# Front loads reordered, decay weights in small tiles, identity products first, the memory norm spread over w_out

## The chip, the cores and the metric

One core of a Trainium2 chip runs the whole kernel. The metric is the time of one execution on the device in microseconds (us); the median of three runs before the change is 1790.62.

## What is computed

The reference is one step of a layer of a hybrid streaming encoder, for 512 prompt tokens and 8 x 16 sample tokens with the same weights, D = 1024, fp32:

```
h = RMSNorm(x);  z = h @ w_in, cut by columns into
  A: band attention (8 heads x 64),   B: gated delta net (4 heads, 128 x 128 state),
  C: Mamba-2 scan (16 heads x 64),    three merge gates g_A, g_B, g_C
x += w_out( sig(g_A) P_A(y_A) + sig(g_B) P_B(y_B) + sig(g_C) P_C(y_C) )
x += CrossAttention(RMSNorm(x), keys and values of RMSNorm(memory))
x += w_down( u * silu(conv(v)) ),  [u, v] = RMSNorm(x) @ w_up
y = RMSNorm(x)
RMSNorm(x) = x * rsqrt(mean(x^2) + eps) * gain
```

The outputs are y, the new attention and memory keys and values, and the states of B, C and the convolutions. Only w_in's column blocks, the normalizations and the last product of w_down are touched by the change.

## The kernel before

The 640 tokens are 5 tiles of 128; D is 8 slices (k) of 128. TensorE (PE) multiplies numbers in fp32r, so every fp32 weight tile is split into a high and a low part: the high part `wh` is a copy by ScalarE (`act`, L249), the low part `wl = raw - wh` a subtraction by GpSimd or VectorE (`tt`, L243). Activations are split in the same way (xTh, xTl). Each product is then three: high by high, low by high, high by low. A weight tile arrives in a "raw" slot (two of them, 512 KB each), its parts lie in "wh"/"wl" slots (six each) or, with `loose=True`, in the general pool "U" of 41 buffers. "Q" is a pool of 16 small tiles (128 x 128). PSUM has two "D" tiles of two banks and four "P" tiles of one bank.

All loads are issued by SyncE (SP) in program order, with a bounded number in flight. The order of the instructions on each engine is fixed when the program is built, by a scheduler that starts from the program's order; inside it, dense parts are generators ("units", `add`, `need`, `drive`) from which the main sequence takes pieces to fill waits.

What the change touches, in the order of the run:

- The front of `run` (from L1801): x tile 0 is loaded, then the gain, then the first four k slices of the V columns of w_in (two raw tiles, `raws`), then x tiles 1 to 4. Tile 0 is normalized and transposed (`norm_T`, L516 on), then tiles 1 and 2, then 3 and 4. Between these, the splits of the V weights are issued. `norm_T` squares x on ScalarE with an accumulated sum (written "junk"), makes 1/rms by 14 short VectorE operations (`inv_rms`: v, y, w, then t, t, y three times), multiplies (xn), transposes xn on PE into PSUM (nps) and copies the parts xTh (ScalarE) and xTl (VectorE). `rel_table` copies the relative bias table, 1 MB as broadcast.
- `decays` (L597): three narrow column blocks of w_in, 32 columns in all, are loaded into one tile "rawd" out of the two raw slots, and PE multiplies them as they are (dps). It is a unit between the first two attention units; aqk is the copy of their products from PSUM, which PE then transposes (t5a).
- `c_norm` (L1207): the outputs yc of branch C are scaled by 1/rms (ScalarE for even token tiles, VectorE for odd ones), transposed (cn, four "P" tiles at a time) and split into ych, ycl. Pieces of a queued unit are taken at its `yield`s; the gate products (gps) of branch C's merge follow.
- `mem_norm` (L1539): the two tiles of memory tokens are normalized ahead of the w_out products (`add_proj`).
- `last_proj` (L1769): the last product of w_down (dn). Its first 512 columns are done first, then x times the final gain on GpSimd for the five token tiles, then the weights of the second 512 columns are split, half of them in loose tiles.

Of the kernel before, what the change touches and what calls it, by code (L numbers as in the profile page):

```python
# [7 lines left out]
F32 = mybir.dt.float32  # L8
F32R = mybir.dt.float32r
I32 = mybir.dt.int32  # L10
AF = mybir.ActivationFunctionType
ALU = mybir.AluOpType
# [21 lines left out]
LQ = 1  # L34
QUARTERS = ((0, 256), (256, 256), (512, 256), (768, 256))
# [9 lines left out]
class Enc:  # L45
# [202 lines left out]
    def act(self, out, in_, f=AF.Copy, **kw):  # L248
        self.nc.scalar.activation(out, in_, f, **kw)  # L249
# [347 lines left out]
    def decays(self, X):  # L597
        nc = self.nc
        w = self.I["w_in"][0]
        raw = self.wp.tile([P, 8, 32], F32, name="rawd", tag="raw", bufs=2)  # L600
        wv = w.rearrange("(k p) c -> p k c", p=P)

        for c, c0, n in ((0, 3072, 8), (8, 6152, 16), (24, 3080, 8)):
            self.load(raw[:, :, c:c + n], wv[:, :, c0:c0 + n])

        ps = self.PD("dps")
        for i in range(2):
            for p in range(2):
                for js in range(2):
                    for j in range(4):  # L610
                        k = 2 * j + i
                        self.mm(ps[32 * j:32 * j + 32, js, :HALF], raw[:, k, :],
# [594 lines left out]
    def c_norm(self, ys, Y):  # L1207
# [4 lines left out]
        yield FN  # L1212
# [326 lines left out]
    def mem_norm(self):  # L1539
        g = self.grow(self.I["norm_mem"][0])  # L1540
        T = [[self.U("mT" + a, F32R, (P, 2, 256)) for _ in range(4)] for a in "hl"]
        for t in range(2):
# [4 lines left out]
            s = slice(t * P, (t + 1) * P)  # L1547
            r = self.token_norm([x])
            for j, ps in self.norm_tile(x, r, g):
                for i in range(2):  # L1550
                    self.act(T[0][2 * j + i][:, :, s], ps[:, 2 * i:2 * i + 2, :])
                for i in range(2):
                    self.tt(T[1][2 * j + i][:, :, s], ps[:, 2 * i:2 * i + 2, :],
                            T[0][2 * j + i][:, :, s].bitcast(F32), ALU.subtract)
        self.MX = [(T[0][k // 2][:, k % 2, :], T[1][k // 2][:, k % 2, :]) for k in range(NK)]

# [212 lines left out]
    def last_proj(self, w, H, x, k0, nk):  # L1769
# [4 lines left out]
        yield from self.add_proj(w, H, x, k0=k0, nk=nk, nm="dn", cols=((0, 512),))  # L1774
# [3 lines left out]
        wk = [a for k in range(0, nk, 2) for a in self.weights(w, 512, 512, k0 + k, 2, (nc.vector, nc.gpsimd), loose=k >= 4)]  # L1778
# [20 lines left out]
    def run(self):  # L1799
# [6 lines left out]
        x0 += [self.load_x(t) for t in range(1, NT)]  # L1806
        self.ident = self.C("ident", [P, P])
        make_identity(self.nc, self.ident)
        self.masks()
# [3 lines left out]
        for c, t in ((0, 1), (1, 3)):  # L1813
            for a in range(2):
                wv += self.split_w(raws[a] if c == 0 else self.raw(w, 1024, 512, 4 + 2 * a, 2), 2, 512, loose=c == 0)
# [9 lines left out]
        self.rel_table()  # L1825
        self.need("A0")
        with self.tc.issue_after(self.last_raw.ins):
            self.loads()
# [168 lines left out]
```

## Time and profile before

| | before |
|---|---|
| runs (us) | 1790.62, 1787.3, 1790.74 |
| median | 1790.62 |
| profiled execution | 1787.08, span 1785.4 |
| mean granted clock of PE | 0.981 |
| PE busy | 1683.1 (94%) |
| VectorE (DVE) busy | 860.4 (48%) |
| ScalarE (ACT) busy | 650.5 (36%) |
| GpSimd (POOL) busy | 607.4 (34%) |
| DMA | 181.78 MB, mean 102 GB/s |

The busy times are sums over the span. PE is busy nearly all of it, so time can come from the stretches in which it waits or runs at a lower clock. Times in the rows below are from the start of the span.

### The profile page before, as it was taken

Reading aid. Unit: us, or ns where it says so; the run is one execution under the profiler, and the core shown is the slowest. Engines: PE = TensorE matmul, PEld = TensorE weight load, DVE = VectorE, ACT = ScalarE, POOL = GpSimd, SP = SyncE. Lnnn points to the kernel's source line nnn. Section 1 sums busy time; section 2 is a strip of 40 time slices with the busy share of each in tenths; the row PEclk is TensorE's granted clock in tenths of the full one; section 3 lists DMA queues with packets and bytes.
Section 4 is the critical chain, followed back from the end, with each engine's and each line's share of the span. In section 5 each row is a group of like instructions: output and inputs, shape, how many; then the busy total and the mean of one; then the engine's idle time right before and its main releaser. Section 6 shows DMA issues by size and latency. Waiting matters only on the chain.

```text
span 1785.4 us, 32450 instructions
## 1 busy us (share of the span) xinstructions
PE 1683.1 (94%) x12925; PEld 1542.6 (86%) x12925; DVE 860.4 (48%) x1762; ACT 650.5 (36%) x1596; POOL 607.4 (34%) x641
## 2 busy tenths in 40 slices
PE   5898999999999998999999899999889999999997
PEld 4687778898988898998899889987789989998995
DVE  5046762446787674755434463243574404431433
ACT  4234543433434432343342245342443313321332
POOL 3252232123322353453432326201144434443432
PEclk9999999999999999999999999999989999999999
DMA  5332156322222334335323345146332222222221
GB/s 177 89 80 66 40 174 197 131 68 64 78 78 67 109 107 113 85 99 145 84 60 119 106 130 166 59 166 236 114 100 74 83 71 83 72 74 82 72 94 61
DMA packets 232749, 181.78 MB, mean 102 GB/s; under 512 B 14321, under 2 KB 198646, under 8 KB 232470
## 3 DMA queue, kind: packets, MB, share of 16 engines
q1 hardware_dynamic: 210672, 165.74, 30.5%
q10 hardware_dynamic: 21926, 13.96, 2.5%
q8 instruction: 102, 1.67, 0.4%
q14 instruction: 49, 0.40, 0.1%
HBM read 163.09 MB, written 16.06 MB: 100 GB/s over the span
## 4 chain that ended last, share of the span: by engine, by line
PE 69%; DVE 10%; DMA 4%; ACT 3%; issue 2%; POOL 1%; ACTq 0%; SPq 0%; POOLq 0%; DVEq 0%
PE ups L235 9%; PE fps L235 9%; PE gps L235 8%; PE dn L235 8%; PE pps L235 6%; PE ap L235 5%; PE tm L235 4%; PE qps L235 3%; PE cps L235 2%; DVE xc L246 2%; PE bps L235 2%; PE pl L235 1%; DVE t L243 1%; PE py L235 1%; PE xkt L240 1%
## 5 line engine op out<-in xcount | busy, mean ns | idle before, releaser
L243 POOL TENSOR_TENSOR wl<-raw,wh 128x512 fp32r<-128x512 f32 x373 | 490.8, 1321 | 961.3 <-ACT wh L249 791.3
L249 ACT ACTIVATE wh<-raw 128x512 fp32r<-128x512 f32 x400 | 248.8, 629 | 591.0 <-PE fps L235 93.8
L246 DVE SCALAR_TENSOR_TENSOR xc<-xp,vec,xc 128x664 f32<-128x664 f32 (+1 forms) x116 | 117.4, 1012 | 3.2
L235 PE MATMUL gps<-xTh,wh 128*128 128x320 f32 x448 | 117.4, 340 | 0.0
L235 PE MATMUL gps<-xTh,wl 128*128 128x320 f32 x448 | 106.3, 315 | 0.0
L235 PE MATMUL gps<-xTl,wh 128*128 128x320 f32 x448 | 105.6, 315 | 0.0
L568 DVE TENSOR_SCALAR xc<-xp,vec 128x656 f32<-128x656 f32 (+1 forms) x34 | 32.2, 948 | 131.9 <-ACT xp L249 131.9
L235 PE MATMUL dn<-wl,hh 128*128 128x512 f32 x220 | 86.4, 394 | 2.9 <-POOL wl L243 2.6
L235 PE MATMUL dn<-wh,hh 128*128 128x512 f32 x220 | 86.3, 393 | 0.1
L235 PE MATMUL dn<-wh,hl 128*128 128x512 f32 x220 | 85.8, 391 | 0.0
L235 PEld LDWEIGHTS gps<-xTh,wh 128*128 128x128 f32 x448 | 74.1, 192 | 12.0 <-issue 10.8
L235 PE MATMUL fps<-fTh,wh 128*128 128x320 f32 x352 | 82.3, 311 | 0.0
L235 PE MATMUL ups<-fTh,wl 128*128 128x320 f32 x352 | 82.0, 310 | 0.0
L235 PE MATMUL fps<-fTl,wh 128*128 128x320 f32 x352 | 81.9, 310 | 0.0
L235 PE MATMUL fps<-fTh,wl 128*128 128x320 f32 x352 | 81.9, 310 | 0.0
L235 PE MATMUL ups<-fTl,wh 128*128 128x320 f32 x352 | 81.8, 310 | 0.0
L235 PE MATMUL ups<-fTh,wh 128*128 128x320 f32 x352 | 81.7, 310 | 0.0
L235 PEld LDWEIGHTS gps<-xTh,wl 128*128 128x128 f32 x448 | 76.0, 190 | 1.0 <-issue 0.8
L235 PEld LDWEIGHTS gps<-xTl,wh 128*128 128x128 f32 x448 | 76.1, 191 | 0.7 <-issue 0.6
L235 PE MATMUL tm<-wh,xTh 128*128 128x256 f32 (+1 forms) x200 | 65.5, 327 | 8.6 <-ACT wh L249 4.4
L243 DVE TENSOR_TENSOR x<-x,dn 128x512 f32<-128x512 f32 x30 | 19.3, 683 | 108.1 <-PE dn L235 107.7
L235 PE MATMUL tm<-wh,xTl 128*128 128x256 f32 (+1 forms) x200 | 63.6, 318 | 0.2 <-DVE xTl L243 0.2
(521 smaller groups left out, 4434.5 us busy)
## 6 DMA issues: line engine op xcount, KB each, us to landing
raw<-in_w_in_dram SPq DMA_DIRECT2D x72, 512.0 KB
raw<-in_w_up_dram SPq DMA_DIRECT2D x44, 512.0 KB
raw<-in_w_down_dram SPq DMA_DIRECT2D x22, 512.0 KB
ck<-in_cache_attn_k_dram SPq DMA_DIRECT2D x32, 256.0 KB
cv<-in_cache_attn_v_dram SPq DMA_DIRECT2D x32, 256.0 KB
xck<-in_cache_mem_k_dram SPq DMA_DIRECT2D x32, 256.0 KB
xcv<-in_cache_mem_v_dram SPq DMA_DIRECT2D x32, 256.0 KB
raw<-in_wx_o_dram SPq DMA_DIRECT2D x14, 512.0 KB
```

The source lines that it names most:

```text
L235: self.nc.tensor.matmul(out, lhsT=lhsT, rhs=rhs, start=start, stop=stop)
L240: self.nc.tensor.transpose(out, in_, self.ident[b:b + k, b:b + k])
L243: return (eng or self.nc.vector).tensor_tensor(out, a, b, op=op)
L246: self.nc.vector.scalar_tensor_tensor(out, a, s, b, op0=op0, op1=op1)
L249: self.nc.scalar.activation(out, in_, f, **kw)
L568: nc.vector.tensor_scalar(acc[:, :n], xp[:, :n], taps[0], bias, op0=ALU.mult, op1=ALU.add)
```

## The change

Five parts:

1. In `run`, the other four k slices of the V weights are loaded right behind x tile 1, into four "U" tiles `rawv`, ahead of x tiles 2 to 4; their splits are issued on ScalarE and GpSimd behind the last ScalarE instruction of tile 0. The relative table is loaded behind the first A0 weights.
2. 14 products of the identity with itself come first on PE.
3. `decays` uses two "Q" tiles and six loads in place of one "raw" tile and three loads.
4. `c_norm` takes 6.5 us' worth of pieces, not 3, at its first `yield`, and one unit of gate products (GD) is queued for it.
5. `mem_norm` is a generator whose steps are spread over w_out's products; `last_proj` splits the weights of its second half ahead of the last k slice of its first half, all but the first two slices in loose tiles.

```diff
--- before.py
+++ after.py
@@ -32,6 +32,7 @@
 LS, LC, LX = 3, 3, 3
 SEQ = (0, 1, 2, 4, 3)
 LQ = 1
+NWARM = 14
 QUARTERS = ((0, 256), (256, 256), (512, 256), (768, 256))
 SKA = 1
 MAGIC = float(0x5F3759DF)
@@ -246,7 +247,7 @@
         self.nc.vector.scalar_tensor_tensor(out, a, s, b, op0=op0, op1=op1)
 
     def act(self, out, in_, f=AF.Copy, **kw):
-        self.nc.scalar.activation(out, in_, f, **kw)
+        self.last_act = self.nc.scalar.activation(out, in_, f, **kw)
 
     def load(self, out, in_):
         return self.nc.sync.dma_start(out, in_)
@@ -597,11 +598,12 @@
     def decays(self, X):
         nc = self.nc
         w = self.I["w_in"][0]
-        raw = self.wp.tile([P, 8, 32], F32, name="rawd", tag="raw", bufs=2)
+        raw = [self.qp.tile([P, 4, 32], F32, name=self.nm("rawd"), tag="Q") for _ in range(2)]
         wv = w.rearrange("(k p) c -> p k c", p=P)
 
         for c, c0, n in ((0, 3072, 8), (8, 6152, 16), (24, 3080, 8)):
-            self.load(raw[:, :, c:c + n], wv[:, :, c0:c0 + n])
+            for i in range(2):
+                self.load(raw[i][:, :, c:c + n], wv[:, 4 * i:4 * i + 4, c0:c0 + n])
 
         ps = self.PD("dps")
         for i in range(2):
@@ -609,7 +611,7 @@
                 for js in range(2):
                     for j in range(4):
                         k = 2 * j + i
-                        self.mm(ps[32 * j:32 * j + 32, js, :HALF], raw[:, k, :],
+                        self.mm(ps[32 * j:32 * j + 32, js, :HALF], raw[k // 4][:, k % 4, :],
                                 X[k][p][:, js * HALF:(js + 1) * HALF].bitcast(F32),
                                 start=(i == 0 and p == 0), stop=(i == 1 and p == 1))
             yield 2.2
@@ -1209,7 +1211,7 @@
         st = self.SM("cst", [P, NT])
         nc.vector.tensor_reduce(st, self.css.rearrange("p a b -> p b a"), axis=AX.X, op=ALU.add)
         r = self.rsqrt(st, 0.25 / D, EPS)
-        yield FN
+        yield 6.5
         for g in range(2):
             for t in (4, 0, 1, 2, 3):
                 if t % 2:
@@ -1537,22 +1539,39 @@
 
 
     def mem_norm(self):
+
         g = self.grow(self.I["norm_mem"][0])
         T = [[self.U("mT" + a, F32R, (P, 2, 256)) for _ in range(4)] for a in "hl"]
+        self.MX = [(T[0][k // 2][:, k % 2, :], T[1][k // 2][:, k % 2, :]) for k in range(NK)]
+
+        def put(t, j, xn):
+            s = slice(t * P, (t + 1) * P)
+            ps = self.PP("nps")
+            for i in range(4):
+                self.tr(ps[:, i * P:(i + 1) * P], xn[:, i * P:(i + 1) * P])
+            ps = ps.rearrange("p (a b) -> p a b", b=P)
+            for i in range(2):
+                self.act(T[0][2 * j + i][:, :, s], ps[:, 2 * i:2 * i + 2, :])
+            for i in range(2):
+                self.tt(T[1][2 * j + i][:, :, s], ps[:, 2 * i:2 * i + 2, :],
+                        T[0][2 * j + i][:, :, s].bitcast(F32), ALU.subtract)
+
+        todo = []
         for t in range(2):
             x = []
             for j in range(2):
                 x.append(self.U("mx", shape=(P, 512)))
                 self.load(x[j], self.I["mem_prompt"][0, t * P:(t + 1) * P, j * 512:(j + 1) * 512])
-            s = slice(t * P, (t + 1) * P)
             r = self.token_norm([x])
-            for j, ps in self.norm_tile(x, r, g):
-                for i in range(2):
-                    self.act(T[0][2 * j + i][:, :, s], ps[:, 2 * i:2 * i + 2, :])
-                for i in range(2):
-                    self.tt(T[1][2 * j + i][:, :, s], ps[:, 2 * i:2 * i + 2, :],
-                            T[0][2 * j + i][:, :, s].bitcast(F32), ALU.subtract)
-        self.MX = [(T[0][k // 2][:, k % 2, :], T[1][k // 2][:, k % 2, :]) for k in range(NK)]
+            for j in range(2):
+                xn = self.U("xn", shape=(P, 512))
+                self.stt(xn, x[j], r, g[j], ALU.mult, ALU.mult)
+                todo.append((t, j, xn))
+            yield
+            for a in todo:
+                put(*a)
+                yield
+            todo = []
 
     def mem_kv(self):
         I, O = self.I, self.O
@@ -1771,11 +1790,14 @@
         nc, O = self.nc, self.O
         g = self.grow(self.I["norm_final"])
         ss = self.SM("fss", [P, 2, NT])
-        yield from self.add_proj(w, H, x, k0=k0, nk=nk, nm="dn", cols=((0, 512),))
+        gen = self.add_proj(w, H, x, k0=k0, nk=nk, nm="dn", cols=((0, 512),))
+        for _ in range(nk - 1):
+            yield next(gen)
+        wk = [a for k in range(0, nk, 2) for a in self.weights(w, 512, 512, k0 + k, 2, (nc.vector, nc.gpsimd), loose=k >= 2)]
+        yield from gen
         for t in range(NT):
             self.sumsq(x[t][0], ss[:, 0, t:t + 1])
             self.tt(x[t][0], x[t][0], g[0], ALU.mult, nc.gpsimd)
-        wk = [a for k in range(0, nk, 2) for a in self.weights(w, 512, 512, k0 + k, 2, (nc.vector, nc.gpsimd), loose=k >= 4)]
         for pair in ((0, 1), (2, 3), (4,)):
             ps = self.PD("dn")
             for j, t in enumerate(pair):
@@ -1803,16 +1825,31 @@
         g = self.grow(I["norm_mix"][0])
         w = I["w_in"][0]
         raws = [self.raw(w, 1024, 512, 2 * a, 2) for a in range(2)]
-        x0 += [self.load_x(t) for t in range(1, NT)]
+        x0.append(self.load_x(1))
+        rawv = [self.U("rawv", shape=(P, 512)) for _ in range(4)]
+        for k in range(4):
+            self.load(rawv[k], w[(4 + k) * P:(5 + k) * P, 1024:1536])
+        x0 += [self.load_x(t) for t in range(2, NT)]
         self.ident = self.C("ident", [P, P])
         make_identity(self.nc, self.ident)
+        warm = self.PP("warm")
+        for _ in range(NWARM):
+            self.mm(warm[:, :P], self.ident, self.ident)
         self.masks()
         X = self.XT("xT")
         all_(self.norm_T(x0, g, X, ((0,),)))
         wv = []
         for c, t in ((0, 1), (1, 3)):
-            for a in range(2):
-                wv += self.split_w(raws[a] if c == 0 else self.raw(w, 1024, 512, 4 + 2 * a, 2), 2, 512, loose=c == 0)
+            if c == 0:
+                tile0 = self.last_act
+                for a in range(2):
+                    wv += self.split_w(raws[a], 2, 512, loose=True)
+            else:
+                with self.tc.issue_after(tile0.ins):
+                    for r in rawv:
+                        h, l = (self.wp.tile([P, 512], F32R, name=self.nm("w" + b), tag="w" + b) for b in "hl")
+                        self.split(h, l, r, self.nc.gpsimd)
+                        wv.append((h, l))
             all_(self.norm_T(x0, g, X, ((t, t + 1),)))
         X = X[1]
         self.m, self.YA, self.V = [], [], None
@@ -1822,9 +1859,9 @@
         self.add("V", self.attn_v(X, wv))
         self.add("A0", self.attn_dense(0, X))
         self.need("V")
-        self.rel_table()
         self.need("A0")
         with self.tc.issue_after(self.last_raw.ins):
+            self.rel_table()
             self.loads()
         self.add("dec", self.decays(X))
         for p in range(1, 4):
@@ -1878,6 +1915,7 @@
         self.need("Z0")
         self.add("Z1", self.z_gate(1, X))
         self.need("Z1")
+        self.add("GD", self.gates(X, w3 + 2048, tc, range(NGC, NGC + 1)))
         Y = []
         self.drive(self.c_norm(self.ys, Y))
         self.add("BC", self.branch(X, lambda: Y, I["w_br_c"][0], w3 + 2048, tc, False))
@@ -1890,8 +1928,12 @@
             self.stt(l, self.m[mt], 0.5, h.bitcast(F32), ALU.mult, ALU.subtract)
             M.append((h, l))
         x = [self.load_x(t) for t in range(NT)]
-        self.mem_norm()
-        all_(self.add_proj(I["w_out"][0], M, x, cols=QUARTERS))
+        mem = self.mem_norm()
+        next(mem)
+        for i, _ in enumerate(self.add_proj(I["w_out"][0], M, x, cols=QUARTERS)):
+            if i % 10 == 9:
+                next(mem, None)
+        all_(mem)
 
         self.add("MK", self.mem_kv())
         to = self.XT("cT")
```

What the engines then have to do at three places, in their own order. SP in the front: before, the last x loads are followed by the relative table and the second pair of V weights (raw_258, raw_268) and the A0 weights (raw_489, raw_552):

```order
L252 DMA x_101<-in_x_prompt_dram 128x512
L252 DMA x_103<-in_x_prompt_dram 128x512
L252 DMA x_105<-in_x_sample_dram 128x512
L252 DMA x_107<-in_x_sample_dram 128x512
L252 DMA relt<-in_a_rel_rev_dram 128x2056
L252 DMA far<-in_a_rel_rev_dram 128x8x1
L252 DMA raw_258<-in_w_in_dram 128x2x512
L252 DMA raw_268<-in_w_in_dram 128x2x512
L252 DMA raw_489<-in_w_in_dram 128x8x128
L252 DMA raw_552<-in_w_in_dram 128x8x128
```

After, rawv_97 to rawv_100 are the same V weights, x_105 to x_107 is token tile 2, raw_504 and raw_567 are the A0 weights:

```order
L253 DMA rawv_97<-in_w_in_dram 128x512
L253 DMA rawv_98<-in_w_in_dram 128x512
L253 DMA rawv_99<-in_w_in_dram 128x512
L253 DMA rawv_100<-in_w_in_dram 128x512
L253 DMA x_105<-in_x_prompt_dram 128x512
L253 DMA x_107<-in_x_prompt_dram 128x512
L253 DMA x_109<-in_x_prompt_dram 128x512
L253 DMA x_111<-in_x_prompt_dram 128x512
L253 DMA x_113<-in_x_sample_dram 128x512
L253 DMA x_115<-in_x_sample_dram 128x512
L253 DMA raw_504<-in_w_in_dram 128x8x128
L253 DMA raw_567<-in_w_in_dram 128x8x128
```

The V weights moved ahead of token tiles 2 to 4, and the table behind the A0 weights.

ScalarE at the channel norm (yc is scaled, ych is copied from the transposes cn, zt belongs to the gate of C). Before:

```order
L249 ACTIVATE zt_10387,css<-yc_9386 128x256
L249 ACTIVATE wh_10703<-raw_10701 128x512
L249 ACTIVATE yc_7759<-yc_7759,yi_10395 128x512
L249 ACTIVATE yc_7454<-yc_7454,yi_10395 128x512
L249 ACTIVATE yc_7646<-yc_7646,yi_10395 128x512
L249 ACTIVATE ych_10424<-cn_10414,vec_664 128x128
L249 ACTIVATE yc_9386<-yc_9386,yi_10395 128x512
L249 ACTIVATE ych_10424<-cn_10419,vec_664 128x512
L249 ACTIVATE yc_9045<-yc_9045,yi_10395 128x512
L249 ACTIVATE ych_10435<-cn_10430,vec_664 128x512
L249 ACTIVATE ych_10435<-cn_10414,vec_664 128x128
L249 ACTIVATE ych_10446<-cn_10441,vec_664 128x512
```

After (tg is the tanh of the gate products gps):

```order
L250 ACTIVATE zt_10410,css<-yc_9409 128x256
L250 ACTIVATE wh_10726<-raw_10724 128x512
L250 ACTIVATE yc_7782<-yc_7782,yi_10418 128x512
L250 ACTIVATE yc_7477<-yc_7477,yi_10418 128x512
L250 ACTIVATE yc_7669<-yc_7669,yi_10418 128x512
L250 ACTIVATE yc_9409<-yc_9409,yi_10418 128x512
L250 ACTIVATE yc_9068<-yc_9068,yi_10418 128x512
L250 ACTIVATE tg_10491<-gps_10432 128x640
L250 ACTIVATE ych_10508<-cn_10498,vec_683 128x128
L250 ACTIVATE ych_10508<-cn_10503,vec_683 128x512
L250 ACTIVATE yc_9296<-yc_9296,yi_10418 128x512
L250 ACTIVATE ych_10519<-cn_10514,vec_683 128x512
```

The first ych moved behind five scalings and a tanh, where it stood behind three scalings.

GpSimd at the end (wl are the splits of the last weights, x the multiplications by the final gain). Before:

```order
L243 TENSOR_TENSOR wl_18985<-raw_18978,wh_18984 128x512
L243 TENSOR_TENSOR wl_19045<-raw_19038,wh_19044 128x512
L243 TENSOR_TENSOR wl_19055<-raw_19048,wh_19054 128x512
L243 TENSOR_TENSOR x_11220<-x_11220,grow_18890 128x512
L243 TENSOR_TENSOR x_11224<-x_11224,grow_18890 128x512
L243 TENSOR_TENSOR x_11228<-x_11228,grow_18890 128x512
L243 TENSOR_TENSOR x_11232<-x_11232,grow_18890 128x512
L243 TENSOR_TENSOR x_11236<-x_11236,grow_18890 128x512
L243 TENSOR_TENSOR wl_19065<-raw_19058,wh_19064 128x512
```

After:

```order
L244 TENSOR_TENSOR wl_19008<-raw_19001,wh_19007 128x512
L244 TENSOR_TENSOR wl_19043<-raw_19036,wh_19042 128x512
L244 TENSOR_TENSOR wl_19033<-raw_19026,wh_19032 128x512
L244 TENSOR_TENSOR wl_19053<-raw_19046,wh_19052 128x512
L244 TENSOR_TENSOR x_11243<-x_11243,grow_18913 128x512
L244 TENSOR_TENSOR x_11247<-x_11247,grow_18913 128x512
L244 TENSOR_TENSOR x_11251<-x_11251,grow_18913 128x512
L244 TENSOR_TENSOR x_11255<-x_11255,grow_18913 128x512
L244 TENSOR_TENSOR x_11259<-x_11259,grow_18913 128x512
```

The last split moved ahead of the five multiplications.

## Rows read from the trace of the kernel before

**Rows 1.** The chain that ended last, shares of the span by engine (page, part 4)
```profile
PE 69%; DVE 10%; DMA 4%; ACT 3%; issue 2%; POOL 1%; ACTq 0%; SPq 0%; POOLq 0%; DVEq 0%
```

**Rows 2.** Windows: stretch, us, busy us of PE, PEld, DVE, ACT, POOL; clock, DMA, GB/s
```profile
12.00:17.00 5.00, 5.00 (x12) 3.42 (x12) 2.71 (x11) 3.39 (x10) 3.17 (x3) 1.00 1.03 386
...
17.00:27.00 10.00, 5.50 (x16) 3.70 (x16) 3.55 (x9) 2.30 (x4) 4.98 (x4) 0.66 0.53 161
...
30.50:42.00 11.50, 8.93 (x47) 7.08 (x46) 9.76 (x24) 4.90 (x12) 2.54 (x2) 1.00 0.26 38
...
78.00:84.00 6.00, 5.40 (x39) 2.81 (x43) 0.28 (x1) 1.71 (x5) 2.00 (x2) 0.50 0.44 109
...
884.00:889.00 5.00, 5.00 (x36) 5.00 (x35) 2.92 (x7) 2.33 (x7) 4.58 (x4) 1.00 0.34 100
...
889.00:897.00 8.00, 5.11 (x29) 4.81 (x28) 5.91 (x17) 5.83 (x11) 1.51 (x1) 0.79 0.28 73
...
1752.00:1761.00 9.00, 6.10 (x20) 4.30 (x19) 1.99 (x2) 1.67 (x4) 5.34 (x4) 0.81 0.00 0
```

**Rows 3.** Timeline, front: start, us, engine, line, operation, count [idle before, releaser]
```profile
10.84 0.63 ACT L249 ACTIVATE wh<-raw 128x512 fp32r<-128x512 f32 x1 [0.20 <-DMA raw<-in_w_in_dram]
...
20.74 1.15 ACT L249 ACTIVATE wh<-raw 128x512 fp32r<-128x512 f32 x2 [5.34 <-DMA raw<-in_w_in_dram]
...
21.42 0.80 PE L235 MATMUL tm<-wh,xTh 128*128 128x512 f32 x1 [4.36 <-ACT wh L249]
```

**Rows 4.** Timeline, VectorE, the chain for token tiles 1 and 2
```profile
15.43 0.16 DVE L243 TENSOR_TENSOR v<-ss 128x2 f32<-128x2 f32 x1 [1.75 <-ACT junk L249]
...
17.99 2.74 DVE L246 SCALAR_TENSOR_TENSOR xn<-x,y,grow 128x512 f32<-128x512 f32 x4
```

**Rows 5.** Timeline, splits on GpSimd and short VectorE operations beside splits
```profile
1001.46 4.99 POOL L243 TENSOR_TENSOR wl<-raw,wh 128x512 fp32r<-128x512 f32 x4 [11.63 <-PE ap L235]
...
1001.52 1.25 DVE L243 TENSOR_TENSOR t<-y,w 128x1 f32<-128x1 f32 x1
...
32.34 1.28 DVE L499 TENSOR_SCALAR y<-y 128x2 int32<-128x2 int32 x1
```

**Rows 6.** Timeline, PE, transposes of token tiles 1 to 4
```profile
26.57 1.04 PE L240 MATMUL nps<-ident,xn 128*128 128x128 f32 x8
...
37.36 0.63 PE L240 MATMUL nps<-ident,xn 128*128 128x128 f32 x4 [2.55 <-DVE xn L246]
```

**Rows 7.** Timeline, the decay weights and the A1 weights
```profile
34.87 1.73 SPq L252 DMA_DIRECT2D rawd<-in_w_in_dram  x3
...
76.81 1.15 ACT L249 ACTIVATE wh<-raw 128x512 fp32r<-128x512 f32 x2 [6.01 <-DMA raw<-in_w_in_dram]
...
78.60 1.12 PE L240 MATMUL t5a<-ident,aqk 128*128 128x128 f32 x4 [6.00 <-ACT aqk L249]
...
84.68 1.51 PE L235 MATMUL dps<-xTl,rawd 128*32 128x320 f32 x15
```

**Rows 8.** Timeline, the channel norm
```profile
891.59 1.93 ACT L249 ACTIVATE yc<-yc,yi 128x512 f32<-128x512 f32 x3
...
892.35 0.65 PE L240 MATMUL cn<-ident,yc 128*128 128x128 f32 x4 [2.89 <-ACT yc L249]
```

**Rows 9.** Timeline, PE, transposes of the second memory tile
```profile
1008.48 0.66 PE L240 MATMUL nps<-ident,xn 128*128 128x128 f32 x4 [4.23 <-DVE xn L246]
```

**Rows 10.** Timeline, the last products and the multiplications on GpSimd
```profile
1749.39 6.73 POOL L243 TENSOR_TENSOR x<-x,grow 128x512 f32<-128x512 f32 x5 [4.45 <-ACT junk L249]
...
1757.39 1.22 PE L235 MATMUL dn<-wl,hh 128*128 128x512 f32 x2 [2.62 <-POOL wl L243]
...
1758.41 0.63 PE L235 MATMUL dn<-wh,hh 128*128 128x512 f32 x1
...
1758.84 0.63 PE L235 MATMUL dn<-wh,hl 128*128 128x512 f32 x1
```

## The prediction

> **What bounds the kernel now.** I read the chain of waits first. It says that TensorE (PE) holds 69% of the chain that ended last and VectorE 10%, DMA 4%, ScalarE 3% [rows 1]. So most of the span is products in a row, which this change leaves as they are, and what it can move is the time in which PE stands still. I then went through PE's groups for "idle before, released by" and cut the stretches around them with the windows view, whose clock column shows what a stop costs afterwards: 1.00 is 2.4 GHz and 0.50 is 1.2 GHz [rows 2]. Five places touch the change. In the front PE waits 4.36 at 21.42 for a weight [rows 3] and 2.55 at 37.36 for a normalized token tile [rows 6]. At 78.60 it waits 6.00 [rows 7], at 892.35 2.89 [rows 8], at 1008.48 4.23 [rows 9], at 1757.39 2.62 [rows 10]. The reader is to see in each who ended the wait, and what stood ahead of that one in its own queue.
>
> **The front.** Before, the last of the first two weight pairs had landed at 10.84 [rows 3], and the bytes come at 386 GB/s with the DMA engines full [rows 2]. Then came the x tiles, and the second half of the weights landed at 20.74. After, x tile 1 (0.52 MB), four weight tiles (1.05 MB) and x tile 2 (0.52 MB) follow on SP: 2.1 MB at 386 GB/s are 5.4 us, so x tile 2 is there at about 16.3. Its two squares follow on ScalarE at the pace of its other 128x512 rows, 0.63 [rows 3], and the chain of 14 short VectorE operations for tiles 1 and 2 starts at about 17.0, where it had started at 15.43 [rows 4]. The weight conversions stand behind the squares on ScalarE, so the first of them ends near 17.5, some 3.2 earlier than at 20.74. Undisturbed, the chain took 17.99 − 15.43 = 2.56 [rows 4], and would end at 19.6.
>
> It will not be undisturbed. From 17.5 GpSimd has six splits in a row, the four of the V weights and two of the first A0 tile, which the change puts right behind them. A split is 4.99 / 4 = 1.25 [rows 5], so they run to 25.0. Where splits ran beside such a chain, one short operation took 1.25 at 1001.52 and 1.28 at 32.34 in place of 0.16 [rows 4, 5]: VectorE gets one operation through per split. Two or three pass before 17.5, six go with the six splits, the rest takes about 0.9: the chain ends at 25.9 and the first xn (2.74 / 4 = 0.69) at 26.6. PE's transposes of these tiles start at 26.57 now [rows 6]. The earlier weights thus buy nothing; PE waits from about 22.5 to 26.6 instead, and the stop costs about 1 us of clock (17 to 27 had 0.66 with 5.5 busy already [rows 2]). The gain is in the next chain, for tiles 3 and 4: it had met two splits, which are then done, so two operations lose 1.1 each, and of the wait of 2.55 about 2.2 goes. Together +2.2 − 1.0, I take +1.3 (gains are positive). The bounds: all of 3.2 + 2.2 + 1.0 = 6.4 if the chain escapes the splits, and −1.5 if one more split or one late x tile stands in it.
>
> The Trainium skill, "SBUF — State Buffer", section "Who interferes with whom", has a rule that speaks against this edit: VectorE shares a port pair with GpSimd, an operation with two SBUF inputs contends for it, and whoever comes first has it for its whole instruction. The trace agrees as far as it goes (1.25 and 1.28 in place of 0.16). By this rule the front is the +1.3 above; without it, +6.4.
>
> The 14 products of the identity need only the identity, and the first transposes wait for the first xn in any case, so they lie in PE's own idle time. They would help by a higher clock later, but the products of tile 0 are already paced by the splits, three products per 1.25, and 12 to 17 had a granted clock of 1.00 [rows 2]. I count 0, between −0.2 and +0.5. The later load of the relative table moves 1 MB out of the front's queue, and I count it with the weights above.
>
> **The decay weights.** The small tile "rawd" took one of the two "raw" slots at 34.87 and its last reader ended at 84.68 + 1.51 = 86.2 [rows 7]. In between the weights had one slot: load, split, load. The conversion at 76.81 waited 6.01 for its load, the eviction aqk stands behind it on ScalarE, and PE waited 6.00 for aqk [rows 7]. Then the clock was 0.50 over 78 to 84, with 39 instructions busy 5.40 [rows 2]: at full clock half of that, and I count 1.9 of the 2.7 as time on the path, as part of the busy time is overlap. After, both slots stand open, the load runs during the earlier split, and the conversion can come up to 6.01 earlier: aqk is ready when PE arrives, at 78.60 − 6.00 = 72.6. What is late next is the split of the same tile on GpSimd; I leave 0.4 for it. So 6.0 + 1.9 − 0.4 = +7.5. The bounds are +8.5 (nothing left over) and +1 (another queue holds aqk back as long). The three more DMA issues lie on SP, which here waits for free slots, so they cost 0.
>
> **The channel norm.** Before, PE waits 2.89 at 892.35 for the scaled yc [rows 8], and 889 to 897 has a clock of 0.79 [rows 2]: 42% of 8 us at half rate are 3.4, of which half, 1.7, is lost. After, 13 more gate products stand ahead of the transposes. In 884 to 889 36 of them took 5.00 [rows 2], so 13 take 1.8 and the wait falls to 1.1. But the transposes now come in one block of 16, and the fourth column group needs a PSUM bank that is read by the first ych. On ScalarE that ych now stands behind five scalings and a gate's tanh where it stood behind three. At 1.93 / 3 = 0.64 each [rows 8] three more are 1.9 us; PE has six products (0.8) to put against it. I take 1.1 for this new wait and 0.4 for smaller ones: 2.89 + 1.7 − 1.1 − 1.1 − 0.4 = +2.0. Bounds +0.5 (the clock falls as before) and +4.6 (both waits hidden).
>
> **The memory norm.** It had stood whole ahead of the first w_out products, and PE waited 4.23 at 1008.48 for its last xn [rows 9]. Four operations of that chain, of which the row at 1001.52 is the first, were held by four splits in a row from 1001.46 to 1006.45 [rows 5]. After, w_out's products are spread around it. The residual adds that now stand in the middle of the second chain wait for the same PE group whose end frees the weight slots, so the chain's rest meets the next splits: 4 x 1.25 again. PE gets there with some 12 products fewer left to do, and these are then done at a lower clock. I take −0.5, bounds −1.5 and +4.2 (the whole wait).
>
> **The tail.** Before, the last split on GpSimd stands behind five multiplications of x, 6.73 from 1749.39, and PE waits 2.62 for it [rows 10]. The clock in 1752 to 1761 is 0.81 [rows 2], and the products at 1758.41 and 1758.84 come 0.43 apart [rows 10], which is 1.2 GHz for 512 columns. After, all splits stand ahead of the multiplications. 2.62 + 1.2 for the clock (38% of 9 us at half rate are 3.4, half is 1.7; part of it is idle) = +3.8, bounds +3.3 and +4.6. The multiplications are needed only when the second half of the last products is evicted, later than they end now. Nothing is late next that I can see.
>
> **The sum.** 1.3 + 0 + 7.5 + 2.0 − 0.5 + 3.8 = 14.1. The profiled execution took 1787.08 (span 1785.4), so 1773.0 on its own time. The three timed runs and it fall into two pairs, 1787.1 and 1787.3, 1790.6 and 1790.7. Their middle, 1788.9, is 1.8 above the profiled one, so I predict 1774.8.
>
> **The rivals.**
> A, the forecast: 1774.8. Chance 0.50.
> B, the chain escapes the splits in the front. For it: the load of the A0 tile lands only around 20 (16.3, and 1.57 MB more at 386 GB/s), so ScalarE could leave gaps. Against it: ScalarE has the conversions in one row, and each split is twice as long. The front gives 6.4 and not 1.3: 1769.7. Chance 0.15.
> C, the change doesn't do what it says at 78.60: aqk is held by another entry of ScalarE's queue, so the slot frees nothing on the path. For it: the conversion that held it still stands near it. The 7.5 go: 1782.3. Chance 0.13.
> D, the waits at the channel norm and at the memory norm go wholly: 2.6 + 4.7 more, 1767.5. For it: most of the products needed to cover them are there. Against it: the queue rows. Chance 0.10.
> E, slower: the block from 22.5 to 26.6 throws PE to 1.2 GHz and it stays there through the V products of the other four tiles, 4 x 24 = 96 of them, at 0.43 instead of about 0.21 apart [rows 10]: 20.6 lost, 1795.4. It decides from 14.1 / 0.215 = 66 products at the low rate. Against it: the 30.5 to 42 stretch holds the wait of 2.55 and has 1.00 [rows 2]. Chance 0.06. The Trainium skill, "TensorE: Matmul & The Clock Gate", section "HAM oscillation — how this bites in real kernels", describes such repeated falls after each wait for data; here the clock came back in the front, so I give it little.
> The last 0.06 are several shortfalls at once, 1784 to 1789.
>
> **How the numbers follow.** The range 1765 to 1783 holds A to D; E and most of the shortfalls stay out. 0.2% is 3.6 us, about what a measurement of this kernel can tell from no change: faster are A to D, 0.88 less a little for their own spread, 0.87; the shortfalls are mostly "same", 0.06; slower is E and the rest, 0.07.
>
> **What would show it.** The steps hold if the profile after has these: PE idle near 22 to 26 released by xn, with VectorE operations of about 1.25 just before; no wait over 1 us near 72 to 75 in front of t5a and a clock of 1.00 there; a wait of about 1 us at the first cn transposes and another before the fourth group; a wait of some 3 to 4 us for the second memory tile's xn; no wait for wl in the last products. The prediction is wrong if PE's first transposes of tiles 1 and 2 come before 24 (B), if t5a still waits over 4 (C), or if the clock is below 0.8 from 27 to 57 (E).

## The result

The changed kernel takes 1766.01 us (median of 4 runs, 1764.74 to 1768.04) against 1788.96 (4 runs, 1786.85 to 1790.74): a ratio of 0.9873, 95% interval 0.9856 to 0.989. Measured again (e8 below) it was 1766.93 against 1790.04, 0.988 (0.9864 to 0.9896). So 21.5 to 23 us are gained where 14.1 were forecast; the time lies in the range, 1.0 above its lower end and 8.8 below the point.

The waits come first. The front, timeline of the changed kernel (start, us, engine, line, operation, count, [idle before, releaser]), beside [rows 3 to 6]:

```profile
17.39 0.16 DVE L244 TENSOR_TENSOR v<-ss 128x2 f32<-128x2 f32 x1 [3.33 <-ACT junk L250]
...
17.99 1.27 DVE L500 TENSOR_SCALAR y<-y 128x2 int32<-128x2 int32 x1
...
24.22 1.19 DVE L244 TENSOR_TENSOR t<-t,y 128x2 f32<-128x2 f32 x1
25.44 0.16 DVE L247 SCALAR_TENSOR_TENSOR y<-t,y 128x2 f32<-128x2 f32 x1
...
17.95 5.00 POOL L244 TENSOR_TENSOR wl<-rawv,wh 128x512 fp32r<-128x512 f32 x4 [2.42 <-ACT wh L250]
22.91 2.48 POOL L244 TENSOR_TENSOR wl<-raw,wh 128x512 fp32r<-128x512 f32 x2
...
27.03 1.97 PE L241 MATMUL nps<-ident,xn 128*128 128x128 f32 x8 [4.30 <-DVE xn L247]
...
37.10 0.63 PE L241 MATMUL nps<-ident,xn 128*128 128x128 f32 x4 [0.79 <-DVE xn L247]
```

GpSimd's six splits run from 17.95 to 25.4, and six operations of the chain take 1.18 to 1.27 each in that time; as soon as the splits end, one takes 0.16 again. PE stands 4.30 for xn.

The decay weights, beside [rows 7], and the tail, beside [rows 10], in the same view:

```profile
67.41 0.63 ACT L250 ACTIVATE wh<-raw 128x512 fp32r<-128x512 f32 x1 [2.03 <-PE aps L236]
70.94 0.63 ACT L250 ACTIVATE wh<-raw 128x512 fp32r<-128x512 f32 x1 [2.90 <-PE aps L236]
71.48 0.69 ACT L250 ACTIVATE aqk<-aps 128x640 f32<-128x640 f32 x1
...
72.27 0.65 PE L241 MATMUL t5a<-ident,aqk 128*128 128x128 f32 x4
...
75.61 1.50 PE L236 MATMUL dps<-xTl,rawd 128*32 128x320 f32 x15
...
1724.26 1.29 POOL L244 TENSOR_TENSOR wl<-raw,wh 128x512 fp32r<-128x512 f32 x1 [3.57 <-ACT wh L250]
1731.58 6.30 POOL L244 TENSOR_TENSOR x<-x,grow 128x512 f32<-128x512 f32 x5 [6.03 <-ACT junk L250]
...
1745.62 0.50 PE L236 MATMUL dn<-wh,hh 128*128 128x512 f32 x1 [0.23 <-DVE x L244]
```

The conversions now wait for PE (a free weight slot), not for a load; t5a waits for nothing, and the dps products come at 75.61 where they came at 84.68. In the tail the last split ends before the multiplications start, and the only wait left is 0.23.

The channel norm, beside [rows 8], and the second memory tile, beside [rows 5, 9]:

```profile
880.80 3.17 ACT L250 ACTIVATE yc<-yc,yi 128x512 f32<-128x512 f32 x5 [1.62 <-DVE yi L247]
...
881.57 1.05 PE L241 MATMUL cn<-ident,yc 128*128 128x128 f32 x6 [1.38 <-ACT yc L250]
...
886.22 0.66 PE L241 MATMUL cn<-ident,yc 128*128 128x128 f32 x4 [1.23 <-DVE ycl L247]
...
991.45 5.42 POOL L244 TENSOR_TENSOR wl<-raw,wh 128x512 fp32r<-128x512 f32 x4 [13.93 <-PE ap L236]
...
990.09 0.42 DVE L244 TENSOR_TENSOR x<-x,ap 128x256 f32<-128x256 f32 x1 [3.31 <-PE ap L236]
990.42 0.15 DVE L247 SCALAR_TENSOR_TENSOR y<-t,y 128x1 f32<-128x1 f32 x1
...
991.60 1.16 DVE L244 TENSOR_TENSOR t<-t,y 128x1 f32<-128x1 f32 x1
992.79 1.19 DVE L247 SCALAR_TENSOR_TENSOR y<-t,y 128x1 f32<-128x1 f32 x1
994.01 3.40 DVE L247 SCALAR_TENSOR_TENSOR xn<-mx,y,grow 128x512 f32<-128x512 f32 x2
...
995.78 0.66 PE L241 MATMUL nps<-ident,xn 128*128 128x128 f32 x4 [2.86 <-DVE xn L247]
```

Both waits of the channel norm are there: 1.38 for the first yc, 1.23 for the fourth group, whose ycl needs the ych that stands behind five scalings in a row. At the memory norm only two operations of the chain are held, and then the two xn.

What the clock made of it, windows of the changed kernel, beside [rows 2] (stretch, us, busy of PE, PEld, DVE, ACT, POOL, clock, DMA share, GB/s):

```profile
24.90:31.70 6.80, 4.67 (x19) 3.80 (x19) 5.88 (x12) 2.93 (x7) 0.49 (x1) 0.50 0.31 27
68.00:74.00 6.00, 6.00 (x55) 4.45 (x57) 0.80 (x1) 2.03 (x5) 2.56 (x2) 1.00 0.33 87
879.00:887.00 8.00, 5.22 (x37) 4.27 (x36) 4.83 (x11) 6.38 (x13) 1.28 (x1) 1.00 0.20 58
990.00:999.00 9.00, 6.14 (x52) 5.94 (x51) 8.12 (x14) 3.79 (x8) 5.42 (x4) 1.00 0.39 113
1034.00:1053.00 19.00, 15.19 (x128) 14.84 (x128) 16.89 (x34) 11.14 (x25) 7.32 (x5) 1.00 0.55 174
1738.00:1747.00 9.00, 8.77 (x39) 6.95 (x38) 4.48 (x18) 2.13 (x6) 0.00 (x0) 1.00 0.01 2
```

These windows are at 1.00 now at four of the five places; the front has a stretch at 0.50 behind its wait, and so has the memory norm's first tile, ahead of its window here.

The same PE product starts at a different time in the two traces; how that lead grows across a place is what the place gained. The last column is the part alone on the kernel before (below), what its ratio gains of 1789:

| place | forecast | lead grows by | part alone, runs (95%) |
|---|---|---|---|
| front (with identity products) | 1.3 | 0.3 | 2.1 (-0.2 to 4.5), and 0.9 (-0.9 to 2.7) |
| decay weights | 7.5 | 8.8 | 9.1 (5.7 to 12.5) |
| channel norm | 2.0 | 1.1 | 0.2 (-2.5 to 2.9) |
| memory norm | -0.5 | 0.7 | 1.6 (-0.9 to 4.1) |
| tail | 3.8 | 4.5 | 5.2 (2.0 to 8.2) |
| sum | 14.1 | 15.4 | 19.1 |
| elsewhere | 0 | 7.0 | |
| whole | 14.1 | 22.4 | 21.5 to 22.7 |

The third column is one pair of profiles, and the other profiles show how firm it is. In all eight that hold the part, the decay weights' place gives 8.8, the tail 4.5 to 4.9 and the channel norm 1.0 to 1.4 (the five without the channel norm's part have -0.6 to 0.2 there). The front and the memory norm are less firm: kernels in which these two places are unchanged differ from before's profile by -0.9 to -0.1 and by -2.1 to -0.5 there. The expectations below put the five places at 15.7 and the rest at 6.7.

### The profile page after: what moved, and what is told of

It is laid out like the page before. It is cut to its first block, busy times and chain, and to the rows that moved or that the text cites. A ratio compares the mean times of both kernels' runs of the same rounds, so it can differ in the third digit from the quotient of the medians.

```text
span 1763.0 us, 32520 instructions
## 1 busy us (share of the span) xinstructions
PE 1678.3 (95%) x12953; PEld 1539.4 (87%) x12953; DVE 867.3 (49%) x1762; ACT 650.0 (37%) x1596; POOL 610.2 (35%) x641
## 4 chain that ended last, share of the span: by engine, by line
PE 69%; DVE 11%; ACT 3%; DMA 3%; issue 2%; POOL 1%; ACTq 0%; SPq 0%; POOLq 0%; DVEq 0%
PE ups L236 9%; PE fps L236 9%; PE dn L236 8%; PE gps L236 8%; PE pps L236 6%; PE ap L236 5%; PE tm L236 5%; PE qps L236 3%; PE cps L236 2%; DVE xc L247 2%; PE bps L236 2%; PE pl L236 1%; DVE t L244 1%; PE py L236 1%; PE t5a L241 1%
## 5 line engine op out<-in xcount | busy, mean ns | idle before, releaser
L236 PEld LDWEIGHTS gps<-xTh,wh 128*128 128x128 f32 x448 | 73.4, 191 | 11.2 <-issue 10.6
L236 PE MATMUL tm<-wl,xTh 128*128 128x256 f32 (+1 forms) x200 | 63.6, 318 | 1.1 <-POOL wl L244 1.1
```

Source lines behind the costliest of these rows:

```text
L236: self.nc.tensor.matmul(out, lhsT=lhsT, rhs=rhs, start=start, stop=stop)
```

## The experiments

**The parts alone.** Each is the kernel before with one part of the diff and nothing else.

```diff
 e1: decays
-        raw = self.wp.tile([P, 8, 32], F32, name="rawd", tag="raw", bufs=2)
+        raw = [self.qp.tile([P, 4, 32], F32, ..., tag="Q") for _ in range(2)]
 e2: mem_norm as a generator, one step per ten of w_out
 e3: last_proj, the second half's splits ahead of the last k slice
 e4: run, rawv loads and splits, rel_table later; no identity products
 e5: c_norm
-        yield FN
+        yield 6.5
+        self.add("GD", self.gates(X, w3 + 2048, tc, range(NGC, NGC + 1)))
```

> The kernel before with the decay weights alone in two small tiles. The forecast's mechanism (one raw slot held for 51 us): no wait ahead of t5a near 78.6 (6.00 before), clock 1.00 behind it, 8 to 9 us gained, as 8.8 were gained at that place in the full change. Rival (the earlier front or the queue on ScalarE did it): the wait stays above 4 and the time within 2 us of before. A second question rides on it: the full change gained 22.4 in the two profiled executions, 15.7 of it at the five places and 6.7 elsewhere, by stretches at 1.2 GHz that are missing. If these hang on the parts, this part alone gains more than 9; if they come and go by execution, it gains 8.8 give or take 3, and its profile has low stretches at other places than either profile has.

1779.0 against 1789.04, ratio 0.9949 (0.993 to 0.9968). t5a starts at 72.62 without a wait. The slot alone carries the term; the rival falls. The second question stays open by the time (9.1, 5.7 to 12.5), but this trace has 0.50 from 114.5 to 121.3, where neither profile of the pair has a low clock. The three timed runs that the forecast rested on made the spread look like 3.5: over these 24 runs the kernel before lies between 1780.74 and 1793.86.

> The kernel before with the memory norm alone spread over w_out. Theory: only its own place changes. There the two waits for xn (1.19 and 4.23 before) become about 2 and 2.9, and the clock stays 1.00 behind the second: about 1 us gained, so 1787 to 1789 as a median. Rival: it is also the cause that the two stretches of 1.2 GHz in the next normalization (1050 and 1067 before) are missing in the full change, then 4 us are gained and both are missing here too.

1786.59 against 1789.04, 0.9991 (0.9977 to 1.0005): the waits are the 1.96 and 2.86 of the theory, and a low stretch still follows the wait at 1050 of this kernel. The rival falls. The stretch at 1067 is missing, but so it is in the other five kernels with one part.

> The kernel before with the last splits alone moved ahead of the multiplications. Nothing runs after this place, so the gain is its own: the wait of 2.62 and the low clock behind it go, 3.8 by the forecast, 4.5 by the full change's profile. Rival (the multiplications or VectorE's splits end last in their turn): a wait for x or for VectorE's wl of over 1 us in the last products, and less than 2 us gained.

1783.42 against 1789.04, 0.9971 (0.9954 to 0.9989). From 1735 on PE's only wait is 0.2 for x. The rival falls.

> The kernel before with the front's loads and splits alone, without the identity products. The forecast's mechanism: six operations of the chain at 1.2 each, transposes at about 27, PE idle some 4 us before them, a wait of about 0.8 in place of 2.55 at the next tiles; net 0 to +1.3 us. If the identity products carry something, this kernel falls behind the full change's front, where V's products were 0.26 ahead of before from 36 us on. Rival (the earlier weights pay): 3 us or more gained.

1787.97 against 1789.04, 0.9988 (0.9975 to 1.0001). The transposes come at 27.33 after a wait of 4.30, the next wait is 0.32, and from 38 us on the lead over before is 0.0. The rival falls by the trace, though the interval alone would allow up to 4.5. The lead is 0.3 under the full change's, but executions differ by more than that here, so no loss without the identity products is shown.

> The kernel before with the channel norm's part alone (6.5 for 3 at the first yield, one more gate unit). Forecast's mechanism: the first wait falls from 2.89 to about 1.1 to 1.4, a new one of 1.1 to 1.3 comes for the fourth group of transposes, released by ych or ycl of the first; 1.1 gained by the full change's profile, 2.0 by the forecast. Rival: the full change's other parts made this place better, then both waits are longer here and nothing is gained.

1788.69 against 1789.33, 0.9999 (0.9984 to 1.0014): not told from nothing. The waits are 1.11 and 1.23, against 1.38 and 1.23 in the full change, so the place does not depend on the other parts; its own lead in this trace is 1.4.

**The identity products.**

```diff
 e6: the changed kernel          e9: the kernel before
-        warm = self.PP("warm")  +        warm = self.PP("warm")
-        for _ in range(NWARM):  +        for _ in range(14):
-            self.mm(...)        +            self.mm(...)   (both cut)
 e8: the changed kernel, no edit
 e11: NWARM = 20
```

> The changed kernel without the 14 identity products. Theory: they carry nothing, within 1 us of the changed kernel (1765 to 1768), and V's products keep their place. Rival: they hold the clock up for the products of token tile 0; then the first 24 products of this kernel take longer, by up to 1.5 us. Second question, the 6.7 us that the change gained outside its five places: if they belong to the change, this kernel is at 1766 to 1768 as well and its profile too lacks the stretches at 1.2 GHz behind the two waits of the next normalization (2.4 and 1.9 long before); if they come and go by execution, some of them are back here and the time lies 2 to 5 us higher.

1772.15 against 1789.33 (6 runs, 1766.73 to 1775.47), 0.9909 (0.9889 to 0.9929): 5 to 6 above the changed kernel, while its profiled execution, one of the fastest of its six (1767.97, span 1766.2), has V's products within 0.7 of the changed kernel's and lacks the stretches in question. Neither theory foresaw that pair, hence the next three.

> The changed kernel itself, on the same chip as the next three, since without the identity products it came out at 1772 (6 runs from 1767 to 1775) where the changed kernel had 1766 (4 runs from 1765 to 1768), though the two profiled executions differ by 0.7 us only up to 1220. Theory one (the identity products carry nothing, the 6 us are executions that fell differently): 1768 to 1774 here, spread as wide. Theory two (they make the later stretches at 1.2 GHz fewer): 1764 to 1768 again, spread under 4.

1766.93 (4 runs, 1765.77 to 1772.16), 0.988. The median is theory two's and the spread theory one's.

> The kernel before with the 14 identity products alone. Theory one: within 1 us of before, with its wide spread (13 us over 41 runs). Theory two: 3 to 6 us faster and a spread under 6.

1789.18 against 1790.04, 0.9995 (0.9985 to 1.0005), 12 runs spread over 9 us. Theory two falls for the kernel before.

> The changed kernel with 20 identity products in place of 14. 14 took 4.78 from 1.53, so 20 end at about 8.4, when the first transposes have their input (8.30). Theory: this place is not on the path, the clock is still 0.50 for the first V products because PE then waits for xTh until 12.4, and the time is that of the changed kernel within 1 us. Rival: with PE busy until the transposes the clock is 1.00 for the products from 12 to 18, and the chain's splits pace them anyway: no gain in time either, but the window shows 1.00.

1768.79, 0.9883 (0.9869 to 0.9898): the same time within the intervals. The window 12 to 18 has a clock of 0.72, as forecast neither by theory nor rival; with 14 products it was 0.74 in one profile (e8) and 0.50 in the other.

**The lock, taken away.** w and t of the chain go into a PSUM bank, so that each operation of the iteration reads one operand from SBUF and not two.

```diff
-        w = self.SM("w", [P, n])
+        wt = self.PP("wt")
+        w, t = wt[:, :n], wt[:, n:2 * n]
...
-        t = self.SM("t", [P, n])
```

> The changed kernel with two of the four small tiles of the 1/rms chain, w and t, in a PSUM bank, so that the nine operations of the iteration have one operand in SBUF each. Theory (an operation with two SBUF operands passes only between two splits): in the front no operation of the iteration takes over 0.4, one or two of the operations before it still take 1.2, the chain ends near 21 and not near 26, the first transposes of tiles 1 and 2 come near 23 in place of 27.03, and the wait of 4.30 falls below 1. The xn multiplications, two SBUF operands each, become held instead. At the memory norm the two held operations go, 2 us earlier. 2 to 5 us gained over the changed kernel: 1761 to 1764. Rival (the chain waits for something else in these stretches, such as SBUF bandwidth taken by the DMA): its operations still take 1.2 and nothing is gained. Rival two: the bank that the chain holds makes PE's transposes wait, and the time is the same or worse.

1759.79 against 1789.33, 0.9844 (0.9824 to 0.9863), 5 to 7 us under the changed kernel and more than the 2 to 5 expected. Its front and its last normalization before w_up:

```profile
18.56 1.26 DVE L500 TENSOR_SCALAR y<-y 128x2 int32<-128x2 int32 x1
19.85 0.17 DVE L244 TENSOR_TENSOR wt<-y,wt 128x2 f32<-128x2 f32 x1
...
21.64 4.54 DVE L247 SCALAR_TENSOR_TENSOR xn<-x,y,grow 128x512 f32<-128x512 f32 x3
...
18.52 5.44 POOL L244 TENSOR_TENSOR wl<-rawv,wh 128x512 fp32r<-128x512 f32 x4 [2.32 <-DMA x<-in_x_sample_dram]
...
24.35 1.03 PE L241 MATMUL nps<-ident,xn 128*128 128x128 f32 x8
...
39.09 0.50 PE L236 MATMUL tm<-wh,xTh 128*128 128x512 f32 x1 [1.18 <-ACT V L250]
...
1292.57 0.63 PE L241 MATMUL nps<-ident,xn 128*128 128x128 f32 x4 [0.91 <-DVE xn L247]
```

The changed kernel at that last place:

```profile
1288.63 1.22 DVE L244 TENSOR_TENSOR t<-t,y 128x1 f32<-128x1 f32 x1
...
1291.38 1.19 DVE L244 TENSOR_TENSOR t<-t,y 128x1 f32<-128x1 f32 x1
...
1294.27 0.69 PE L241 MATMUL nps<-ident,xn 128*128 128x128 f32 x4 [3.89 <-DVE xn L247]
```

While the splits run, the iteration's operations take 0.17, and only y<-y and the xn, which stay in SBUF, are held (4.54 for three). That is the lock shown by taking it away; rival one falls. The Trainium skill, "SBUF — State Buffer", section "Who interferes with whom", says that an operation with at most one SBUF input outside the two-port modes does not contend; the 0.17 beside a running split agree. y<-y has one operand in SBUF, not two, and is held all the same, so two operands are not the only case.

The gain is not where it was expected: in the front the transposes come 2.7 earlier, but a wait of 1.18 for the eviction of V takes the place of the old one, and from 50 us on the lead is -0.4 here, 0.9 in e10 and 0.4 in e12, no more than the -0.4 to 0.7 of four profiles without PSUM tiles (the changed kernel twice, e6, e11). That is not rival two: the tile that PE waits for is a "D" tile, not the bank of the chain. The gain came at the memory norm, where the wait of 2.86 is gone (the lead grows by 3.0, against 0.7 to 2.1 in these four), and in the normalization ahead of w_up, where the wait fell from 3.89 to 0.91 (the lead grows by 6.3, and by 3.3 in e10 below, against -1.6 to 1.5 in the four). Part of it was lost earlier: at 880 of before's time the lead is 8.7 here and 5.9 in e10, against 10.6 to 12.1 in the four; whether the PSUM tiles or the executions do that was not settled.

```diff
 e10: e7 without the identity products
 e12: e7, and in run
+        mem = self.mem_norm()
+        next(mem)
         self.need("BC")
...
-        mem = self.mem_norm()
-        next(mem)
```

> The kernel with w and t of the 1/rms chain in PSUM, without the identity products. Theory one: 1759 to 1761, as with them. Theory two: 1763 to 1767, with a wider spread.

1762.93 against 1790.04, 0.9847 (0.9829 to 0.9865), 4 runs from 1756.71 to 1765.44. The median lies between the theories, the spread is theory two's, and its interval holds e7's ratio: undecided.

> The kernel with w and t of the 1/rms chain in PSUM, and the first step of the memory norm (its first tile's xn) moved ahead of the last products of branch C. Theory: the wait of 1.98 for that xn at the start of w_out goes, and the low clock behind it (a stretch from 984): 2 to 3 us gained over 1759.8, so 1757 to 1758. Rival: its ten or so buffers are taken earlier from the pool and something else waits for them, or its splits and copies fall on ScalarE's and VectorE's busiest stretch of the merge: 1759 or slower.

1758.95 against 1788.62, 0.9835 (0.9816 to 0.9853). The waits for both memory tiles are gone, PE is busy without a break from 970 to 1000 (two windows, 15.00 of 15.00 each), and that stretch gained 7.7 of lead (3.0 in e7); 0.8 is left in the median, and the profiled span, 1757.6, equals e7's. The theory's 2 to 3 is not shown, since the intervals overlap; this profile entered the stretch 3.5 behind e7's (a lead of 6.3 at 935, against 9.8). Its median is the lowest here, clear of the changed kernel and not of e7.

## Why the prediction was right, and where it was short

The range held, and the mechanisms of the front, the decay weights, the channel norm and the tail are in the trace; the sum was some 8 too small, one step of the memory norm failed, and one reading of the clock was wrong. That the time stayed in the range, by 1.0, is in part luck: 7.0 of the gain came from stretches for which the forecast had no term.

**Front.** The lock, the count of six held operations, the wait (22.5 to 26.6 forecast, 22.7 to 27.03 found) and the shrinking of the other wait are as forecast. The term was mis-sized, mostly by the clock: counted at 1.0, the stretch at 0.50 from 24.9 covers the transposes themselves, so tile 1's products start at 30.97 and not at 29.44, 1.5 later. Of the wait of 2.55, 1.8 went and not 2.2. Instead of +1.3 (the forecast's own terms make 1.2) it was +0.3. Of the two rows that the forecast took for operations with two SBUF inputs, the one at 32.34 (1.28) is y<-y, which has one.

**Identity products.** The forecast read 1.00 in 12 to 17 [rows 2] as full speed paced by splits. That reading was wrong. In the kernel before the products come 0.43 apart, the 1.2 GHz step of [rows 10], and 0.23 apart only from about 16 on, while the column has 1.00 throughout:

```profile
14.60 0.63 PE L235 MATMUL tm<-wl,xTh 128*128 128x512 f32 x1
15.03 0.63 PE L235 MATMUL tm<-wh,xTh 128*128 128x512 f32 x1
...
16.20 0.40 PE L235 MATMUL tm<-wh,xTh 128*128 128x512 f32 x1
16.43 0.40 PE L235 MATMUL tm<-wh,xTl 128*128 128x512 f32 x1
```

The changed kernel without identity products (e6) has 1.00 and 0.43 there too:

```profile
12.00:18.00 6.00, 4.92 (x11) 3.61 (x12) 1.38 (x2) 4.65 (x13) 4.24 (x4) 1.00 1.03 371
```

```profile
14.40 0.63 PE L235 MATMUL tm<-wl,xTh 128*128 128x512 f32 x1
14.82 0.63 PE L235 MATMUL tm<-wh,xTh 128*128 128x512 f32 x1
15.25 0.63 PE L235 MATMUL tm<-wh,xTl 128*128 128x512 f32 x1
```

With the identity products the column has 0.50, after a wait of 2.29 for xTh, and the products come 0.43 apart as well, so they gained nothing here:

```profile
12.00:18.00 6.00, 5.62 (x13) 3.84 (x13) 1.93 (x7) 4.60 (x13) 3.58 (x4) 0.50 1.06 378
```

The term of 0 stands on the kernel before (e9). On the changed kernel the ratios with and without them differ by 5 us in one pair (e8 and e6, whose intervals just overlap) and by 0.5 in the other (e7 and e10), without a place in the traces that shows it: that stays open.

**Decay weights.** Right; mis-sized by the two deductions, 0.4 for a leftover and 0.8 of the clock. Nothing was left over and the whole 2.7 came back: 6.0 + 2.7 = 8.7 against 8.8.

**Channel norm.** Both waits were forecast at 1.1 and are 1.38 and 1.23; with one of 0.17 between them PE stands 2.78 where it stood 2.89, so the waits gave 0.1. The other 1.0 of the 1.1 is the clock, and its 1.7 was the mis-sized term. The slow stretch of before lies wholly behind the wait (893.3 to 896.7, PE busy 3.40 of 3.40, clock 0.50), so why it gave 1.0 and not 1.7 is open. In time the part alone can't be told from nothing; the traces show it.

**Memory norm.** The step that failed is "the chain's rest meets the next splits: 4 x 1.25 again". The residual add was released at 990.09, the chain resumed at 990.42, a microsecond before the first split (991.45), and only its last two operations met them. The wait for the second tile is 2.86 and not 4.23, and no low clock follows (in e8 one does), where before had 3.4 us at 0.50: about 3 gained. That only 0.7 of it is left in the pair lies at the first tile, which the forecast did not price. Its wait, before's line first, then the changed kernel's and the window around it:

```profile
992.24 0.66 PE L240 MATMUL nps<-ident,xn 128*128 128x128 f32 x4 [1.19 <-DVE xn L246]
...
980.69 1.11 PE L241 MATMUL nps<-ident,xn 128*128 128x128 f32 x4 [1.95 <-DVE xn L247]
...
976.50:984.50 8.00, 6.05 (x39) 5.84 (x38) 5.29 (x19) 2.25 (x7) 1.02 (x1) 0.79 0.56 191
```

The change need not be the cause: this wait is 1.95 to 1.97 in the five kernels whose memory norm is unchanged, and 1.19 again in e8.

**Tail.** Right; the whole 1.7 of the clock came back, and 0.2 more.

**Elsewhere.** The forecast had no term for it, and it is the largest miss: 7.0 in the profiled pair. One part repeats. In the next normalization, after the memory keys, the lead grows by 3.3 to 3.5 in all seven profiles of kernels with the five places changed, and by 0.4 to 1.9 in the six with one part. As this place is unchanged in those six, some 1.4 of the 3.5 (their mean) is that before's own profile was slow there. The first wait there is 2.11 to 2.26 in the seven and 2.24 to 2.95 in the six; what differs is that a slow stretch follows in all six and in none of the seven. The channel norm alone (e5), and the changed kernel again (e8), each the wait and the window behind it:

```profile
1053.93 0.92 PE L240 MATMUL nps<-ident,xn 128*128 128x128 f32 x4 [2.24 <-DVE xn L246]
```

```profile
1054.00:1058.00 4.00, 4.00 (x22) 4.00 (x23) 2.58 (x6) 1.20 (x2) 0.00 (x0) 0.57 0.46 141
```

```profile
1036.40 0.63 PE L241 MATMUL nps<-ident,xn 128*128 128x128 f32 x4 [2.23 <-DVE xn L247]
```

```profile
1036.00:1040.00 4.00, 3.60 (x31) 3.63 (x32) 3.94 (x9) 2.18 (x4) 0.31 (x1) 1.00 0.62 200
```

After the wait of 2.24 the clock fell, after that of 2.23 it did not, so length alone doesn't decide. Which part of the change, or only the sum of its shifts, brings this about was not settled. The other 3.5 come and go between executions: at 1340 of before's time the lead of the changed kernel was 17.8 in one profile and 14.8 in the other. With the parts' sum of 19.1, each good to some 3 us, the whole 21.5 to 22.7 leaves nothing that must be explained by more than these, and doesn't exclude it.

The forecast's time was nearer to rival D's 1767.5 than to its own, but D's mechanism, both waits gone, did not happen: 1.38, 1.23 and 2.86 are still there.

## What to carry to other kernels

A small buffer that lives long must not sit in a pool whose slots the big loads turn over: one slot held for 51 us cost 9. Short chains on VectorE beside long splits on GpSimd pay one split per operation, and putting one operand of each two-operand operation into PSUM takes that away. When a wait goes, price the low clock behind it: two of the three places gave it back in full, the channel norm 1.0 of 1.7. Read the spacing of the products, not the clock column alone.

## What was not expected of the hardware

The clock column can say 1.00 while products of 512 columns come 0.43 apart: here at the start of an execution, up to about 16 us in the kernel before and 18 in that of e6. A wait of 2.24 was followed by 1.2 GHz in e5 and one of 2.23 was not in e8. The kernel before spread over 13 us (1780.74 to 1793.86, 24 runs), the mean granted clock going with the time: 0.986 in the fastest of these runs and 0.978 in the slowest. A VectorE operation with a single SBUF operand (y<-y) was held beside a split as well (1.26).
